# Later stores, paired weight loads, earlier heads and a sixth load buffer in one step of a retention/HGRN2 decoder layer

## The chip, the cores and the metric

The kernel runs on one core of one Trainium2 chip. The metric is the device time of one execution in microseconds; where several runs are given, it is their median. All of the time is in one launch.

## The reference, cut to what matters

The reference computes one inference step of one hybrid decoder layer (model width 1024), for one prompt of 2048 tokens with zero state and for 8 sample sequences of 8 tokens that bring a state each. Both share the weights:

```
proj = rmsnorm(x) @ w_in                      # 1024 x 4096
rq, rk, rv, rg, hq, hf, hi, hg = split(proj)  # 8 parts of 512 columns, 4 heads of 128 each
o_r = retention(rotary(rq), rotary(rk), rv)   # S = gamma_h * S + k v^T   , o = q S
o_h = hgrn2(silu(hq), 1 - f, hi, log f)       # S = diag(f) * S + (1-f) i^T, o = q S
o   = [head_rmsnorm(o_r) * silu(rg), head_rmsnorm(o_h) * silu(hg)]
x   = x + o @ w_out                           # 1024 x 1024
x   = x + square(relu(rmsnorm(x) @ w_up)) @ w_down     # 1024 x 4096, 4096 x 1024
y   = rmsnorm(x)
```

The outputs are y for prompt and samples and the final states of the 8 heads, for the prompt and for each sample sequence. Everything is in float32. The recurrences are computed in chunks: inside a chunk by products of queries and keys with a decay between them, across chunks by the state.

## The kernel before, in words

**Groups and layout.** The 2112 tokens are cut into three groups of 640 (prompt), 768 (prompt) and 704 (64 sample tokens and 640 of the prompt), worked through one after the other. Activations lie with features on the 128 partitions and tokens along the free axis, in "slabs" of 128 x 768. The mixing of all three groups (input projection, heads, output projection) comes before the three feed-forward passes, which begin at about 1170 us and multiply block matrices with fewer products by way of sums of weights (`plan_sums`, L1272) that are made beforehand, during the mixing.

**Weights in two parts.** Each 128 x 1024 weight tile is loaded into one of four `raw` buffers on SyncE's queue (L233), cast by ScalarE into a high part `hi` (L268) and subtracted by VectorE into a low part `lo` (L282, in `second_part`, four ticks after the cast). Activations have two parts as well, and each product is three matmuls: high by high, high by low, low by high. `weight(i)` makes sure that weight i is there, and brings up as many more as `self.ahead` says; `hi` and `lo` have five buffers each (`NPART`). `next_weight` hands out the next weight of the stream. For weights 4 to 35 of the first group it also stores both parts to DRAM at once (L315-316, on SyncE's queue, so the queue waits there until the low part is made); groups two and three load these parts back (L253) and do not split them again.

**Order of the work.** `mix(g)` runs over four pairs of heads, one retention head and one HGRN2 head each. For a pair, `project` makes queries, keys and forget gates (four blocks, rotary tables applied at L705-L706), `mixer` writes the side work of the pair on an agenda, and `values` (L739-L745) multiplies the tokens by the pair's four value weights (`N_VAL`). `proj` calls `tick()` after each pair of matmuls of a block's two halves, `values` after two of each three of its matmuls; `at(t, ...)` and `later(t, ...)` place a piece of side work t ticks ahead, so it is issued between the matmuls of that moment. Three 512-column matmuls of `values` are two ticks, 16 ticks a chunk of 128 tokens. Each engine then works its instructions in the order in which the program issued them (a scheduler may move them within that). The agenda of a pair holds the corner products of the HGRN2 decay levels (L983, copied out by ScalarE at L986, their exponents made on GpSimd at L901 and ScalarE at L905), the sums for the next token (their operand made at L504, the products' result taken over at L970), the retention scores (L1040, taken over by VectorE at L1041), turned keys, outputs and states.

**Heads.** When a pair's outputs exist, `cut_heads` (L1215-L1232) turns them to feature layout for the output projection: for each of its two heads and two or three chunk trios a transpose on TensorE (L1229) into a PSUM tile of the pool `mm`, which has four, then the high part on ScalarE (L1230) and the low part on VectorE (L1231). Heads of pairs 0, 1 and 2 are turned during the last pair, at ticks 50, 65 and 80; those of the last pair at its end.

**Sample states.** In the third group, `sample_states` (L775) loads each head's eight states in two halves into buffers of the pool `ld`, which has five (`NLD`), is shared with the rotary tables and the operands of the weight sums, and also holds the new states until they are stored (L849).

**The first weights.** The whole start of the kernel runs on little data: the normalising factor of the first group (`rsqrt`, L355-L356, on ScalarE), the rotary tables multiplied by it (L592, GpSimd), the first projections multiplied by it (L643, VectorE) or by the tables (L705, VectorE, which reads the PSUM tile, and L706, GpSimd), and the first blocks of weights, all within some 41 us.

Of the kernel before, what the change touches and what calls it, by code (L numbers as in the profile page):

```python
# [9 lines left out]
F32 = mybir.dt.float32  # L10
# [5 lines left out]
P = 128  # L16
# [4 lines left out]
SLEN = 8  # L21
NS = NSEQ * SLEN
# [5 lines left out]
C = 128  # L28
SLAB = 768
NSLAB = 43  # L30
NLD = 5
NRAW = 4
NPART = 5
LEVELS = (64, 32, 16, 8, 4, 2)

MASKS = (16, 8, 4, 2, "odd", 1, 0)
SMASKS = (4, 2, "odd", 1, 0)
NMSK = len(MASKS) * P + len(SMASKS) * NS
GAM = [1.0 - 2.0 ** (-5.0 - h) for h in range(H)]


# [12 lines left out]
N_VAL = 4  # L54
# [60 lines left out]
def constants():  # L115
    c = np.zeros((P, NCONST), np.float64)
    c[:, C_ID:C_ID + P] = np.eye(P)
    s = np.arange(P)[:, None]
    t = np.arange(P)[None, :]
    sc = DK ** -0.5  # L120
    same = (s // SLEN == t // SLEN) & (s < NS) & (t < NS)
    for h, g in enumerate(GAM):
        dec = np.where(s <= t, g ** np.maximum(t - s, 0), 0.0) * sc
        c[:, C_RM + h * P:C_RM + (h + 1) * P] = dec
        c[:, C_RS + h * NS:C_RS + (h + 1) * NS] = np.where(same, dec, 0.0)[:, :NS]
        c[:, C_GQ + h * P:C_GQ + (h + 1) * P] = g ** (t + 1.0)
        c[:, C_GS + h * NS:C_GS + (h + 1) * NS] = g ** (np.arange(NS) % SLEN + 1.0)
        c[:, C_KS + h] = sc * g ** (P - 1.0 - s[:, 0])
        c[:, C_KSS + h] = sc * g ** (SLEN - 1.0 - s[:, 0] % SLEN)
    c[:, C_SM:C_SM + 4] = (s % 32 // SLEN == np.arange(4)[None, :])  # L130
    def mask(w):
        if w == "odd":
            return mask(2) * (s % 2)
        return s == t if not w else (s // (2 * w) == t // (2 * w)) & (s % (2 * w) < w) & (t % (2 * w) >= w)

    m = np.concatenate([mask(w) for w in MASKS] + [(mask(w) * (s < NS))[:, :NS] for w in SMASKS], 1)
    half = DK // 2
    inv = np.power(10000.0, (-np.arange(half, dtype=np.float32) / np.float32(half)).astype(np.float64)).astype(np.float32)
    pos = in_groups(np.tile(PAST + np.arange(SLEN), NSEQ), np.arange(SEQ)).astype(np.float32)
    ang = (inv[:, None] * pos[None, :]).astype(np.float64)  # L140
    cs = np.zeros((P, 2, NT), np.float32)
    cs[:half, 0] = cs[half:, 0] = np.cos(ang)
    cs[:half, 1] = -np.sin(ang)
    cs[half:, 1] = np.sin(ang)
    return c.astype(np.float32), m.astype(np.uint8), cs.reshape(P, -1)
# [54 lines left out]
class Kernel:  # L200
# [108 lines left out]
    def next_weight(self):  # L309
        i = self.w_use  # L310
        self.w_use += 1
        r = self.weight(i)
        if N_MADE <= i < N_KEPT:
            self.kept[i] = [self.dp.tile([P, WT], F32, name=f"w{i}{part}") for part in ("hi", "lo")]
            for part, kept in zip(r, self.kept[i]):  # L315
                self.nc.sync.dma_start(kept, part.bitcast(F32))
        self.wts.pop(i - 4, None)
        return r

    def take(self, n):  # L320

# [53 lines left out]
    def build(self):  # L375
        nc, tc, I = self.nc, self.tc, self.I
        with ExitStack() as ctx:
# [33 lines left out]
            self.eps, self.eps_h = eps[:, 0:1], eps[:, 1:2]  # L411
            self.con, self.vec, self.msk = con, vec, msk
            self.mask = {w: msk[:, i * P:(i + 1) * P] for i, w in enumerate(MASKS)}
            self.smask = {w: msk[:, len(MASKS) * P + i * NS:len(MASKS) * P + (i + 1) * NS] for i, w in enumerate(SMASKS)}
            self.ident = con[:, C_ID:C_ID + P]

            gs = []
# [13 lines left out]
            self.ahead = 2  # L431
            self.weight(0)

            self.reset = cp.tile([P, P + NS], F32, name="reset")
            nc.gpsimd.memset(self.reset, 1.0)
            nc.gpsimd.memset(self.reset[:, P:].rearrange("p (c t) -> p c t", t=SLEN)[:, :, 0:1], 0.0)
            self.S = cp.tile([P, 2 * H, P], F32, name="S")
            self.AT = [cp.tile([P, 3, P], F32, name=f"AT{i}") for i in range(2)]
            for a in self.AT:
# [181 lines left out]
    def mix(self, g):  # L621
        nc = self.nc
        if g.ns:
            g.qm = [self.get(), self.get()]
            for q in g.qm:
                nc.gpsimd.memset(q, 0.0)
        g.o, g.oc = {}, {}
        end = 0
        for p in range(H):
            b = {}  # L630
            self.project(g, p, b)
            end = self.mixer(g, p, b, max(self.now, end))
            if p == H - 1:
                for q in range(H - 1):
                    self.later(50 + 15 * q, self.cut_heads, g, q)
            self.values(g, p, b)

    def block(self, g):
# [71 lines left out]
    def values(self, g, p, b):  # L710


        nc, n = self.nc, len(g.starts)
        ahead, self.ahead = self.ahead, NPART - N_VAL
        w = [self.next_weight() for _ in range(N_VAL)]
        self.ahead = ahead
        b["vs"], b["vc"], b["gate"] = None, [], []
        trios, left, i1 = [], -(-n // 3), 0
        while left:
            i0, i1 = i1, i1 - (i1 - n) // left  # L720
            left -= 1
            trios.append((i0, i1))
        g.trios = trios
        slabs = {}
        for j0 in range(0, n, 2):
            pj = self.pj.tile([P, 2, 512], F32, tag="pj", name="pjv")
            part = g.starts[j0:j0 + 2]
            for i, s in enumerate(part):
                dst = pj[:, i]
                for kb in range(KB):  # L730
                    hh, hl = g.h[kb]
                    cols = slice((kb % 2) * 512, (kb % 2 + 1) * 512)
                    wh, wl = (a[:, cols] for a in w[kb // 2])
                    if g.ns and s == 0:

                        last = kb == KB - 1
                        for q in (1, 0) if last else (0, 1):
                            if q:
                                nc.tensor.matmul(dst[:NS], hh[:, :NS], wl, start=False, stop=False, skip_group_check=True)  # L739
                            else:  # L740
                                nc.tensor.matmul(dst, self.hs[:, kb * P:(kb + 1) * P], wh, start=kb == 0, stop=last)
                        self.tick()
                        continue
                    for q, (a, ww) in enumerate(((hh, wh), (hh, wl), (hl, wh))):
                        nc.tensor.matmul(dst, a[:, s:s + C], ww, start=kb == 0 and q == 0, stop=kb == KB - 1 and q == 2)  # L745
                        if q != 1:
                            self.tick()
            for i, s in enumerate(part):
                j = j0 + i
                k = next(k for k, (a, e) in enumerate(trios) if a <= j < e)  # L750
                if k not in slabs:
                    slabs[k] = self.get(), self.get()
                c0 = (j - trios[k][0]) * 256
                for t, c in ((slabs[k][0], 0), (slabs[k][1], 256)):
                    nc.scalar.activation(t[:, c0:c0 + 256], pj[:, i, c:c + 256], AF.Copy, scale=g.rt[:, j:j + 1])
                v, z = (t[:, c0:c0 + 256] for t in slabs[k])
                b["gate"].append(z)
                if g.ns and s == 0:
                    b["vs"], b["vrows"] = (v[:, :P], v[:, P:]), v[:NS]
                    low = self.load()[:NS, :512]  # L760
                    for h, t in enumerate((v, z)):
                        nc.sync.dma_start(low[:, h * 256:(h + 1) * 256], t[NS:])
                        self.later(16 + h, lambda t=t, r=low[:, h * 256:(h + 1) * 256]: nc.vector.tensor_tensor(
                            out=t[:NS], in0=t[:NS], in1=r, op=ALU.add))
                else:
                    b["vc"].append((v[:, :P], v[:, P:]))
                if j == trios[k][1] - 1:
                    self.gates(slabs[k][1], c0 + 256, 22 if g.ns and trios[k][0] == 0 else 4)
# [97 lines left out]
    def mixer(self, g, p, b, t0):  # L866
# [15 lines left out]
        def scans():  # L882
            lf, bb = x["lf"], x["bb"]
            for c in cols:
                nc.vector.tensor_tensor_scan(out=bb[:, c], data0=self.reset[:, :C], data1=lf[:, c], initial=0.0,
                                             op0=ALU.mult, op1=ALU.add)
            if n0:
                nc.vector.tensor_tensor_scan(out=bb[:, :NS], data0=self.reset[:, P:], data1=lf[:, :NS], initial=0.0,
                                             op0=ALU.mult, op1=ALU.add)


# [269 lines left out]
        at(14, next_products)  # L1161
        at(22, next_keys)
        at(25, next_parts)
        at(50, next_to)
        for i, w in enumerate(LEVELS):
            t = 6 + step * i
            at(t, exponents, w)
# [5 lines left out]
            for sg in (parts if 2 < w < SLEN else range(2)):  # L1173
                at(t + late + 3 * sg + (wait if w == 2 else 9 if w >= 32 else 4), level, i, sg)
        for sg in parts:
            at(46 + 4 * sg, ret_scores, sg)
            at(60 + 4 * sg, turn, "ktr", rk, sg, C_KS)
        at(60, ret_queries)
        t = 6 + step * len(LEVELS)
# [677 lines left out]
```

## Time and profile before

| | |
|---|---|
| median of 3 runs | 2503.9 us (2501.46 to 2505.31) |
| the profiled execution's own time | 2503.73 us |
| its span in the profile | 2501.9 us |
| granted TensorE clock, mean | 0.997 |
| instructions | 39554 |
| TensorE busy | 99% of the span |
| VectorE, ScalarE, GpSimd busy | 73%, 49%, 15% |
| moved by DMA | 525.6 MB, 210 GB/s |

The profile is of one execution. Lines such as "PE pjv L745 <- DVE slab L705: 3.4, 1, 3.4" say that TensorE's matmuls of line 745, into the tile pjv, were idle before their start for 3.4 us in all, once, and that what ended the idle time was VectorE's instruction of line 705. In lists of single instructions the columns are start, duration, engine, line, operation, result and operands, the number of instructions in the row, and in brackets the idle time ahead of it with its releaser. "SPq" is SyncE's queue, which issues transfers. In tables by stretch, "PEclk" is the clock that TensorE was granted, as a share of full speed.

### The profile page before, as it was taken

The numbers are of one execution on the slowest core, as the hardware profiler recorded it, in microseconds if no ns is written. First come the engines' busy times: TensorE is split into PE (matmuls) and PEld (weight loads), VectorE is DVE, ScalarE is ACT, GpSimd is POOL, SyncE is SP. The second block draws the span as 40 slices with busy tenths as digits, with TensorE's granted clock in tenths as the row PEclk, the third lists the DMA queues.
The fourth block names the chain that finished last, engine by engine and source line by source line (L and its number), as shares of the span: only waits on it lengthen the run. The fifth ranks groups of instructions, "written<-read, shape, count | busy, mean of one in ns | idle before, by whom it ended". The sixth has DMA issues, their size and how long they took to land.

```text
span 2501.9 us, 39554 instructions
## 1 busy us (share of the span) xinstructions
PE 2481.5 (99%) x15408; PEld 2379.1 (95%) x15408; DVE 1814.2 (73%) x2449; ACT 1221.5 (49%) x1966; POOL 380.1 (15%) x320
## 2 busy tenths in 40 slices
PE   9999999999999999999999999999999999999998
PEld 8999898998899889989999999999999999999998
DVE  7666766557583656666775899786688878778997
ACT  6565653444463444443644555544454436445443
POOL 4223304324321443340000000000000000000000
PEclk9999999999999999999999999999999999999999
DMA  7544464645465566747866856566675555867652
GB/s 279 203 180 174 165 240 152 250 177 196 178 229 228 191 207 228 249 179 250 292 225 211 283 199 211 187 231 227 202 252 181 181 163 181 292 198 244 205 184 97
DMA packets 191968, 525.57 MB, mean 210 GB/s; under 512 B 21027, under 2 KB 62883, under 8 KB 191782
## 3 DMA queue, kind: packets, MB, share of 16 engines
q1 hardware_dynamic: 191638, 523.03, 60.8%
q8 instruction: 121, 1.98, 0.3%
q14 instruction: 65, 0.53, 0.1%
q10 hardware_dynamic: 144, 0.02, 0.0%
HBM read 389.28 MB, written 132.39 MB: 209 GB/s over the span
## 4 chain that ended last, share of the span: by engine, by line
PE 92%; DVE 2%; POOL 2%; DMA 1%; ACT 1%; issue 1%; SPq 0%; DVEq 0%; POOLq 0%; ACTq 0%
PE pf L1240 26%; PE pj L1240 25%; PE pj L339 20%; PE pjv L745 12%; PE mm L926 2%; PE mm L1108 1%; PE mm L1110 1%; PE mm L1116 1%; DMA raw<-w 1%; PE mm L983 1%; PE mm L1229 1%; PE mm L856 1%; PE mm L790 1%; PE mm L1040 1%; POOL slab L901 0%
## 5 line engine op out<-in xcount | busy, mean ns | idle before, releaser
L268 ACT CAST hi<-raw 128x1024 fp32r<-128x1024 f32 x392 | 411.8, 1051 | 608.3 <-PE pf L1240 242.1
L1240 PE MATMUL pf<-slab,hi 128*128 128x320 f32 (+2 forms) x2768 | 657.8, 321 | 0.0
L1240 PE MATMUL pj<-slab,hi 128*128 128x352 f32 (+2 forms) x2608 | 620.7, 322 | 0.0
L282 DVE TENSOR_TENSOR lo<-raw,hi 128x1024 fp32r<-128x1024 f32 x392 | 482.9, 1233 | 120.8 <-ACT hi L268 116.0
L339 PE MATMUL pj<-slab,hi 128*128 128x320 f32 (+2 forms) x2304 | 486.6, 327 | 0.8 <-DVE slab L1300 0.8
L1240 PEld LDWEIGHTS pf<-slab,hi 128*128 128x128 f32 x2768 | 480.1, 188 | 0.0
L1240 PEld LDWEIGHTS pj<-slab,hi 128*128 128x128 f32 x2608 | 452.9, 188 | 0.1
L1240 PE MATMUL pf<-slab,lo 128*128 128x320 f32 (+2 forms) x1384 | 444.2, 321 | 0.0
L1240 PE MATMUL pj<-slab,lo 128*128 128x352 f32 (+2 forms) x1304 | 419.2, 321 | 0.0
L339 PEld LDWEIGHTS pj<-slab,hi 128*128 128x128 f32 x2304 | 382.0, 188 | 5.0 <-issue 1.9
L745 PE MATMUL pjv<-hi,slab 128*128 128x512 f32 x1024 | 349.1, 403 | 3.4 <-DVE slab L705 3.4
L339 PE MATMUL pj<-slab,lo 128*128 128x320 f32 (+2 forms) x1152 | 282.3, 326 | 0.1
L1240 PEld LDWEIGHTS pf<-slab,lo 128*128 128x128 f32 x1384 | 259.7, 188 | 0.0
L1240 PEld LDWEIGHTS pj<-slab,lo 128*128 128x128 f32 x1304 | 244.7, 188 | 0.0
L745 PEld LDWEIGHTS pjv<-hi,slab 128*128 128x128 f32 x1024 | 194.1, 190 | 40.3 <-DVE slab L705 3.6
L745 PE MATMUL pjv<-lo,slab 128*128 128x512 f32 x512 | 206.7, 404 | 0.0
L339 PEld LDWEIGHTS pj<-slab,lo 128*128 128x128 f32 x1152 | 198.3, 188 | 0.5 <-DVE lo L282 0.4
L1331 ACT CAST slab<-slab 128x640 fp32r<-128x640 f32 (+2 forms) x192 | 145.2, 778 | 69.5 <-DVE slab L1342 50.4
L1335 DVE TENSOR_TENSOR slab<-slab 128x640 fp32r<-128x640 f32 (+2 forms) x192 | 166.8, 887 | 13.4 <-PE pf L1240 6.6
L905 ACT ACTIVATE slab<-slab 128x640 f32<-128x640 f32 (+2 forms) x72 | 56.3, 782 | 125.0 <-POOL slab L901 124.1
L745 PEld LDWEIGHTS pjv<-lo,slab 128*128 128x128 f32 x512 | 97.1, 190 | 15.3 <-DVE lo L282 0.3
L1585 DVE TENSOR_TENSOR slab<-pf,slab 128x640 f32<-128x640 f32 (+2 forms) x88 | 77.7, 888 | 22.0 <-PE pf L1240 21.5
(231 smaller groups left out, 2959.5 us busy)
## 6 DMA issues: line engine op xcount, KB each, us to landing
raw<-w SPq DMA_DIRECT2D x264, 512.0 KB, 4.6
slab<-u SPq DMA_DIRECT2D x32, 384.0 KB, 5.0
u<-ld SPq DMA_DIRECT2D x30, 384.0 KB, 4.3
slab<-u SPq DMA_DIRECT2D x32, 352.0 KB, 5.1
u<-ld SPq DMA_DIRECT2D x30, 352.0 KB, 4.4
slab<-u SPq DMA_DIRECT2D x32, 320.0 KB, 4.5
u<-ld SPq DMA_DIRECT2D x30, 320.0 KB, 4.0
ld<-x SPq DMA_DIRECT2D x16, 384.0 KB, 4.0
```

What stands on the lines that cost most here:

```text
L268: self.nc.scalar.copy(hi, raw)
L282: self.nc.vector.tensor_tensor(out=lo, in0=self.second.pop(j), in1=hi.bitcast(F32), op=ALU.subtract)
L339: self.nc.tensor.matmul(pj[:, i, :T2], w, a[:, c0:c1], start=j == 0 and q == 0, stop=j == n - 1 and q == 2)
L745: nc.tensor.matmul(dst, a[:, s:s + C], ww, start=kb == 0 and q == 0, stop=kb == KB - 1 and q == 2)
L790: nc.tensor.matmul(po, g.qm[i][:, s * NS:(s + 1) * NS], s0[i][:, s * P:(s + 1) * P], start=False, stop=i == 1 and s == 3)
L856: nc.tensor.transpose(ps[:, j * P:(j + 1) * P], src[:, c], self.ident)
L905: nc.scalar.activation(x["dd", w][:, a:T], x["dd", w][:, a:T], AF.Exp)
L926: nc.tensor.matmul(ps[:, j], qk[:, cols[c]], second(qk[:, cols[c]]), start=True, stop=True)
L1240: self.nc.tensor.matmul(*a, **k)
L1331: self.nc.scalar.copy(hi[:, :g.T], B[name][:, :g.T])
L1335: self.nc.vector.tensor_tensor(out=lo[:, :g.T], in0=B[name][:, :g.T], in1=hi.bitcast(F32)[:, :g.T], op=ALU.subtract)
L1585: nc.vector.tensor_tensor(out=r, in0=ps, in1=r, op=ALU.add)
```

## The change

Six edits, all in the order and the buffers of the work; no product and no arithmetic is added or left out.

1. The stores of the weights kept for the later groups go on the agenda ten ticks ahead (`keep`), and are no longer issued at the moment when a weight is handed out.
2. `values` asks for the pair's last but one value weight, with those that `self.ahead` adds, in one call before it takes the four.
3. Heads of pairs 0, 1 and 2 are turned at ticks 4, 16 and 28 of the last pair, not 50, 65 and 80.
4. The pool `ld` has six buffers instead of five.
5. Inside the pair's agenda the next-token sums go to tick 45 (from 50) and the retention scores to 48 + 4 sg (from 46 + 4 sg).
6. The masks of the sample tokens are cut from those of the prompt, so the mask table that is loaded has 896 columns instead of 1216; the scans read an existing tile of ones, and the tile of ones and zeros for the samples' scans loses its 128 columns of ones.

```diff
-NLD = 5
+NLD = 6
...
-NMSK = len(MASKS) * P + len(SMASKS) * NS
+NMSK = len(MASKS) * P
...
         if N_MADE <= i < N_KEPT:
             self.kept[i] = [self.dp.tile([P, WT], F32, name=f"w{i}{part}") for part in ("hi", "lo")]
-            for part, kept in zip(r, self.kept[i]):
-                self.nc.sync.dma_start(kept, part.bitcast(F32))
+            self.later(10, self.keep, r, self.kept[i])
         self.wts.pop(i - 4, None)
         return r
+
+    def keep(self, parts, kept):
+        for part, k in zip(parts, kept):
+            self.nc.sync.dma_start(k, part.bitcast(F32))
...
-            self.reset = cp.tile([P, P + NS], F32, name="reset")
+            self.reset = cp.tile([P, NS], F32, name="reset")
...
             if p == H - 1:
                 for q in range(H - 1):
-                    self.later(50 + 15 * q, self.cut_heads, g, q)
+                    self.later((4, 16, 28)[q], self.cut_heads, g, q)
             self.values(g, p, b)
...
         ahead, self.ahead = self.ahead, NPART - N_VAL
+        self.weight(self.w_use + N_VAL - 2)
         w = [self.next_weight() for _ in range(N_VAL)]
...
-                nc.vector.tensor_tensor_scan(out=bb[:, c], data0=self.reset[:, :C], data1=lf[:, c], initial=0.0,
+                nc.vector.tensor_tensor_scan(out=bb[:, c], data0=self.ones, data1=lf[:, c], initial=0.0,
...
-        at(50, next_to)
+        at(45, next_to)
...
-            at(46 + 4 * sg, ret_scores, sg)
+            at(48 + 4 * sg, ret_scores, sg)
```

More of the change, by code (lines that the diff above doesn't have):

```diff
@@ L36 @@
 MASKS = (16, 8, 4, 2, "odd", 1, 0)
-SMASKS = (4, 2, "odd", 1, 0)
-NMSK = len(MASKS) * P + len(SMASKS) * NS
+NMSK = len(MASKS) * P
 GAM = [1.0 - 2.0 ** (-5.0 - h) for h in range(H)]
@@ L134, in mask @@
         return s == t if not w else (s // (2 * w) == t // (2 * w)) & (s % (2 * w) < w) & (t % (2 * w) >= w)
-    m = np.concatenate([mask(w) for w in MASKS] + [(mask(w) * (s < NS))[:, :NS] for w in SMASKS], 1)
+    m = np.concatenate([mask(w) for w in MASKS], 1)
     half = DK // 2
@@ L413, in build @@
             self.mask = {w: msk[:, i * P:(i + 1) * P] for i, w in enumerate(MASKS)}
-            self.smask = {w: msk[:, len(MASKS) * P + i * NS:len(MASKS) * P + (i + 1) * NS] for i, w in enumerate(SMASKS)}
+            self.smask = {w: m[:, :NS] for w, m in self.mask.items() if w != "odd" and w <= SLEN // 2 or w == "odd"}
             self.ident = con[:, C_ID:C_ID + P]
@@ L432, in build @@
             self.weight(0)
-            self.reset = cp.tile([P, P + NS], F32, name="reset")
+            self.reset = cp.tile([P, NS], F32, name="reset")
             nc.gpsimd.memset(self.reset, 1.0)
-            nc.gpsimd.memset(self.reset[:, P:].rearrange("p (c t) -> p c t", t=SLEN)[:, :, 0:1], 0.0)
+            nc.gpsimd.memset(self.reset.rearrange("p (c t) -> p c t", t=SLEN)[:, :, 0:1], 0.0)
             self.S = cp.tile([P, 2 * H, P], F32, name="S")
@@ L884, in scans @@
             for c in cols:
-                nc.vector.tensor_tensor_scan(out=bb[:, c], data0=self.reset[:, :C], data1=lf[:, c], initial=0.0,
+                nc.vector.tensor_tensor_scan(out=bb[:, c], data0=self.ones, data1=lf[:, c], initial=0.0,
                                              op0=ALU.mult, op1=ALU.add)
             if n0:
-                nc.vector.tensor_tensor_scan(out=bb[:, :NS], data0=self.reset[:, P:], data1=lf[:, :NS], initial=0.0,
+                nc.vector.tensor_tensor_scan(out=bb[:, :NS], data0=self.reset, data1=lf[:, :NS], initial=0.0,
                                              op0=ALU.mult, op1=ALU.add)
```

## The prediction

> **What bounds the kernel now.** I read the page first, then who TensorE waited for, then the granted clock in narrow stretches around the longest waits, then each engine's instructions in order of time at those places.
>
> ```profile
> PE 2481.5 (99%) x15408; PEld 2379.1 (95%) x15408; DVE 1814.2 (73%) x2449; ACT 1221.5 (49%) x1966; POOL 380.1 (15%) x320
> ...
> L1240 PE MATMUL pf<-slab,hi 128*128 128x320 f32 (+2 forms) x2768 | 657.8, 321 | 0.0
> ```
>
> TensorE is busy for 2481.5 of 2501.9 us, and the feed-forward products (L1240), which fill the span from about 1170 us on, wait for nothing. The change removes no matmul. So all it can win is idle time of TensorE in the first half, and what hangs on it.
>
> ```profile
> engine line waited for: us in total, times, longest us
> PE pjv L745 <- DVE slab L705: 3.4, 1, 3.4
> PE mm L1229 <- DVE slab L1041: 1.8, 1, 1.8
> PE mm L790 <- DMA ld<-hg_s: 1.6, 2, 1.4
> PE mm L1040 <- ACT AT L986: 1.3, 3, 0.6
> ...
> PE mm L1229 <- DVE AT L970: 0.4, 1, 0.4
> PE mm L983 <- DVE slab L912: 0.3, 1, 0.3
> ```
>
> These waits lie before 1200 us. Five places, 8.8 us in all, are ones that the edits touch: the first value product (3.4), the early heads of the last group's last pair (1.8 and 0.4), the states of the sample sequences (1.6), retention scores in the second group (1.3), one corner product (0.3). Two of them cost more than their idle time:
>
> ```profile
> core 0: us, PE busy (x), PEclk, DMA share, GB/s
> 36.50:41.30 4.80, 1.45 (x8) 1.00 1.03 327
> 41.30:44.80 3.50, 3.50 (x10) 0.51 0.72 286
> ...
> 1092.70:1096.00 3.30, 1.08 (x7) 1.00 1.03 322
> 1096.00:1099.50 3.50, 3.50 (x18) 0.51 0.99 365
> ```
>
> Behind both stalls the granted clock is 0.51 for 3.5 us, so half of that, about 1.7 us, is lost again each time. The ceiling is 8.8 + 3.4 = 12.2 us.
>
> **The change part by part.** Stores ten ticks later, and a pair's value weights asked for together: this is the first stall.
>
> ```profile
> 27.87 0.33 SPq L316 DMA_DIRECT2D w4lo<-lo  x1
> 28.24 0.43 SPq L233 DMA_DIRECT2D raw<-w  x1
> ```
>
> ```profile
> 28.67 0.51 ACT L355 ACTIVATE slab<-mm,eps 128x320 f32<-128x320 f32 x1
> 33.08 1.05 ACT L268 CAST hi<-raw 128x1024 fp32r<-128x1024 f32 x1 [3.91 <-DMA raw<-w]
> 34.03 0.47 ACT L356 ACTIVATE slab<-slab 128x320 f32<-128x320 f32 x1
> ```
>
> ```profile
> 17.06 1.23 DVE L282 TENSOR_TENSOR lo<-raw,hi 128x1024 fp32r<-128x1024 f32 x1 [1.96 <-ACT hi L268]
> ...
> 26.62 2.36 DVE L282 TENSOR_TENSOR lo<-raw,hi 128x1024 fp32r<-128x1024 f32 x2
> ...
> 35.30 4.28 DVE L643 TENSOR_TENSOR slab<-slab 128x640 f32<-128x640 f32 x2
> 39.51 0.81 DVE L705 TENSOR_TENSOR slab<-pj,ld 128x640 f32<-128x640 f32 x1
> ```
>
> ```profile
> 36.57 0.46 PE L339 MATMUL pj<-slab,lo 128*128 128x320 f32 x2
> 40.37 0.50 PE L745 MATMUL pjv<-hi,slab 128*128 128x512 f32 x1 [3.35 <-DVE slab L705]
> ```
>
> Read backwards: TensorE waits for a PSUM buffer that L705 frees at 40.32. L705 needs the rotary table, which needs the whole normalising factor. Its second half (L356) stands on ScalarE behind a weight cast (L268) that waits 3.91 us for a load. SyncE could issue that load (third value weight) only at 28.24, since the store of w4's low part, ahead of it on its queue, waited for w4's subtraction, the first of the two in the row at 26.62, and so went at 27.87. In the new order three loads precede the stores. The load then goes when its buffer is free, with the subtraction that ends at 17.06 + 1.23 = 18.3, and lands 33.08 - 28.24 = 4.8 us later, at 23.1. Its cast (1.05) now stands ahead of L355 and is done by about 25.3; L356 follows at 28.67 + 0.51 and ends at 29.7, not 34.5. The cast of the fourth value weight comes behind it, so nothing is late there.
>
> From 34.50 to 40.32 the rest of the chain took 5.8 us: it would end at 35.5. But the order puts the low part of the fourth value weight ahead of L705. That adds 1.2 us (17.06), or about twice as much if GpSimd slows it as it slowed the L643 pair: 36.7 to 38.1. TensorE is through its block at 36.9. A stall of 0 to 1.2 us is left; I take 0.7, near the middle, since GpSimd's table work runs at that time. With no 3 us gap I expect no slow stretch. The gain is 3.4 - 0.7 + 1.7 = 4.4 us, between 3.9 and 5.1. The corner product's 0.3 goes too: its chain starts some 5 us earlier, TensorE 4.4. The delayed stores keep their buffers 10 ticks (about 3.4 us) longer, and SyncE's queue then holds them behind three loads; the next user of such a buffer comes five weights later, so the wait lies beside matmuls (if that cover went, a cast would be late by 3.4 us).
>
> ```profile
> 34.58 4.32 POOL L592 TENSOR_TENSOR ld<-ld,slab 128x640 f32<-128x640 f32 x2 [10.62 <-ACT slab L356]
> 38.98 2.00 POOL L706 TENSOR_TENSOR slab<-slab,ld 128x640 f32<-128x640 f32 x1
> ```
>
> Two L643 took 4.28 us while GpSimd ran L592. The Trainium skill, "SBUF — State Buffer", section "SBUF: two separate sides", says that a VectorE instruction with two SBUF inputs and a GpSimd instruction share a port pair that one of them holds for its whole instruction. By that rule the fourth low part stands behind L706 (2.00) whenever GpSimd starts first, and the stall left is 1.2 us and the sum 0.5 us smaller; if VectorE starts first it is 0. The trace agrees as far as the doubled L643 shows.
>
> Six load buffers: the states.
>
> ```profile
> 872.93 0.42 SPq L849 DMA_DIRECT2D hg_so<-ld  x1
> ...
> 874.54 0.39 SPq L775 DMA_DIRECT2D ld<-hg_s  x1
> ```
>
> The second hg_s load of a pair waited for a buffer and went out behind the state stores; TensorE needed it at once. In the new order both hg_s loads of a pair stand ahead of all four state stores, over 10 us earlier. I count the whole 1.6 us. Beyond 1170 us the sixth buffer only moves operand loads forward, where TensorE has no wait (L1240, 0.0): nothing.
>
> Ticks 45 and 48: the retention scores.
>
> ```profile
> 501.09 0.85 ACT L905 ACTIVATE slab<-slab 128x768 f32<-128x768 f32 x1 [2.09 <-POOL slab L901]
> ```
>
> ```profile
> 502.19 0.94 PE L1040 MATMUL mm<-slab 128*128 128x128 f32 x6 [0.37 <-ACT AT L986]
> ```
>
> The second score product needs the PSUM tile that L986 frees, which stands behind a decay that waits for GpSimd. Two ticks are 0.7 us (three 512-column matmuls), more than the longest of these waits (0.6). The 1.3 us go. The next-token sums come 5 ticks, 1.7 us, earlier; their operand (L504) is done over 3 us before in such a pair, so nothing is added there.
>
> Heads at ticks 4, 16 and 28: the last pairs.
>
> ```profile
> core 0: us, PE busy (x) PEld busy (x) DVE busy (x) ACT busy (x) POOL busy (x), PEclk, DMA share, GB/s
> 655.00:672.00 17.00, 17.00 (x84) 13.66 (x83) 12.80 (x16) 6.40 (x11) 12.63 (x9) 1.00 0.86 310
> 1071.00:1089.00 18.00, 18.00 (x85) 13.95 (x84) 13.92 (x17) 6.32 (x11) 13.13 (x10) 1.00 0.36 137
> ```
>
> ```profile
> 668.84 0.56 PE L983 MATMUL mm<-slab 128*64 128x64 f32 x6
> ...
> 676.39 1.47 PE L1229 MATMUL mm<-con,slab 128*128 128x128 f32 x12
> ...
> 1085.53 0.45 PE L983 MATMUL mm<-slab 128*64 128x64 f32 x4
> ```
>
> ```profile
> 677.54 2.19 DVE L1231 SCALAR_TENSOR_TENSOR slab<-mm,vec,slab 128x384 fp32r<-128x384 f32 x4 [0.39 <-ACT slab L1230]
> ...
> 1116.45 2.07 DVE L1231 SCALAR_TENSOR_TENSOR slab<-mm,vec,slab 128x320 fp32r<-128x320 f32 x4 [0.40 <-ACT slab L1230]
> ```
>
> The work is the same; only the place moves. In the last group the old place cost 1.8 + 0.4 + 1.7 = 3.9 us. The new place puts three batches of four evacuations (2.2, 2.1 us of VectorE each, and about as much of ScalarE) into a stretch where VectorE is busy for 13 of 17 us. All four PSUM tiles go to a batch, so what follows on TensorE waits for VectorE. TensorE itself reaches the first corner product (L983) later by three batches of 1.4 us, 4.2 us. Second group: up to L504 VectorE has about 11 us of work from 657.4, with the batches 17.8, end 675.2, first tile free 1.6 earlier at 673.6; TensorE comes at 668.84 + 4.2 = 673.0, so 0.6 us is lost. Last group: the steps in the new order add to 19 us from 1073.0, first tile free at 1090.5 against 1085.53 + 4.2 = 1089.7: 0.8 us, and then about 0.9 us for the tile of the next-token sums, whose mask copies stand behind two more products of the next decay level. First group, with no weight sums on VectorE: 0. Bounds for the three together: 0 (GpSimd, freed of the overlap with weight sums, delivers its exponents earlier) and 5 us (VectorE's idle time all filled, 2 us each in two groups, 1 in the first). I take 2.3.
>
> At nothing: the smaller mask load (its first reader is 20 us behind it), scans that read the tile of ones (same instruction and size), the shorter memset before the first matmuls.
>
> **The sum**, against the profiled execution's 2503.7 us (span 2501.9; the median of the runs is 2503.9, the same): 4.4 + 0.3 + 1.6 + 1.3 + 3.9 - 2.3 = 9.2 us. Forecast 2494.5 us.
>
> **The rivals.** (1) *The first stall stays for the most part.* L705 also waits for GpSimd's tables, and doubled VectorE and GpSimd instructions could push it out by 3 us; the slow stretch comes back. Against it: that chain starts 4.8 us earlier. Then 3.4 + 1.7 of the gain go, less what the earlier loads still save (1): 2498.6. (2) *New waits in the last pairs take back what the old ones gave.* For it: 12.8 to 13.9 us of VectorE work already there. At the far end 5 us are lost, and stalls of 2.2 us within 3.4 us were enough for a slow stretch at 1096, so two such add 3.4: 12.2 - 0.7 - 8.4, 2500.6, within 0.2%. (3) *Slower:*
>
> ```profile
> 664.50 0.85 ACT L905 ACTIVATE slab<-slab 128x768 f32<-128x768 f32 x1 [6.27 <-POOL slab L901]
> ```
>
> ScalarE holds a batch's evacuation behind a decay that waits for GpSimd (here it idled 6.27 us for one). If each later batch waited for one such decay, TensorE would lose about 4 us twice in each of three pairs, with a slow stretch of 1.7 behind each pair: 3 x (8 + 1.7) = 29, less 11.5 won: 2521. It decides from about 4 us per pair and batch; the order has the decay ahead of the second batch, but TensorE reaches the third batch some 5 us later, which covers it. (4) *Better:* no new wait and no stall left at the start, 12.2: 2491.5, and with smaller waits of the same stretch gone (0.8 at 351, 0.6 at 1158) 2490. That the edits don't act is excluded by the instruction order, which shows the loads and the heads moved.
>
> The Trainium skill, "TensorE: Matmul & The Clock Gate", section "Part 1: The HAM clock gate (the "warmup" mystery)", lets the clock fall only after an idle window of about 3.4 us. The row 1092.70:1096.00 speaks otherwise: TensorE was busy for 1.08 of 3.30 us and the clock fell. By the page rival 2 would cost 3.4 us less, 2497.2.
>
> **How the numbers follow.** Forecast, 2491.8 to 2498: 0.66. Rival 1: 0.10. Rival 2: 0.12. Rival 3: 0.03. Rival 4: 0.09. 0.2% (5 us) is about what a measurement of this kernel can tell from no change. Faster by over 0.2% means under 2498.7: the forecast, rival 4, half of rival 1 and a fifth of rival 2 give 0.82. Slower: rival 3 and a little for the unforeseen, 0.04. Within: 0.14. The range takes in rival 4, the forecast, rival 1 and most of rival 2: 2489.5 to 2500.5.
>
> **What would show it.** After: no wait of the first value product over 1.3 us and a clock of 1.00 at 41 us; the third value load issued near 18 us and L356 done near 30; no wait for hg_s; no slow stretch near 1096, and the waits at L983 or L1229 of the last pairs under 1 us each. A new wait of TensorE for L1231's tiles of over 2 us in a pair, or a clock of 0.5 in a last pair, would make it wrong; so would a first stall that only moved to another releaser.

## The result and the profile after

The changed kernel takes 2490.97 us (median of 4 runs, 2490.0 to 2491.32) against 2503.13 us before (4 runs, 2501.46 to 2505.31): ratio 0.995, 95% interval 0.9933 to 0.9968. That is 12.2 us where 9.2 were forecast; it lies inside the range, below the forecast's own range (2491.8 to 2498), at the number of rival 4 (2491.5). The interval is a gain of 8 to 17 us, so the times alone do not tell 9.2 from 12.2; the terms have to be checked in the traces. The profiled span went from 2501.9 to 2489.4 us, by 12.5.

Busy times of the changed kernel, part 1 of its page, and then whom TensorE waited for:

```profile
PE 2475.5 (99%) x15408; PEld 2376.1 (95%) x15408; DVE 1807.9 (73%) x2449; ACT 1223.6 (49%) x1966; POOL 372.6 (15%) x320
```

```profile
engine line waited for: us in total, times, longest us
PE mm L408 <- DVE eps L412: 1.1, 1, 1.1
PE pj L341 <- DVE slab L1303: 0.8, 1, 0.8
PE mm L1113 <- DVE S L1126: 0.7, 1, 0.7
PE mm L512 <- DVE slab L506: 0.6, 1, 0.6
PE pjv L748 <- DVE slab L707: 0.5, 1, 0.5
PE pj L341 <- DVE lo L281: 0.4, 1, 0.4
PE pf L1787 <- ACT slab L1778: 0.4, 1, 0.4
PE mm L816 <- ACT slab L813: 0.4, 1, 0.4
PE pj L341 <- ACT hi L267: 0.2, 1, 0.2
```

Lines are those of the changed kernel, two or three above the old ones. The list adds up to 5.1 us, before to 11.9. The first value product (L748, before L745) waits 0.5 and not 3.4 us; the waits for sample states, for the PSUM tiles of turned heads and for the scores are not in the list at all. Four short waits, 1.6 us together, are new in the list: L512 (0.6), L816 (0.4) and two of L341 for the parts of a weight (0.4 and 0.2). TensorE has the same 15408 matmuls and 6.0 us less busy time; about 3.4 us of that is the half clock, since no stretch runs at it any more (stretches of the changed kernel, columns as before):

```profile
core 0: us, PE busy (x) PEld busy (x) DVE busy (x) ACT busy (x) POOL busy (x), PEclk, DMA share, GB/s
37.00:41.00 4.00, 3.48 (x17) 2.73 (x16) 3.72 (x5) 3.92 (x6) 2.74 (x3) 1.00 1.03 402
41.00:45.00 4.00, 4.00 (x20) 3.30 (x19) 3.17 (x8) 1.47 (x2) 1.46 (x2) 1.00 0.98 345
...
1090.00:1096.00 6.00, 6.00 (x44) 4.95 (x43) 2.96 (x7) 1.72 (x5) 2.46 (x4) 1.00 0.60 189
1096.00:1100.00 4.00, 4.00 (x22) 3.40 (x21) 0.59 (x3) 0.14 (x2) 0.00 (x0) 1.00 0.00 0
```

So 6.8 us of listed waits and about 3.4 us of half clock make 10.2 of the 12.5 us. The other 2.3 are not gaps: TensorE's idle time fell by only 6.5 us (20.4 to 13.9), no more than the listed waits. They are matmuls that last less at a clock of 1.00 in both kernels (6.0 - 3.4 = 2.6 us of busy time); why is not taken apart.

The first stall went as the prediction had it. SyncE's queue, then VectorE, in the changed kernel:

```profile
15.60 12.84 SPq L232 DMA_DIRECT2D raw<-w  x4
28.50 0.42 SPq L320 DMA_DIRECT2D w4hi<-hi  x1
```

```profile
30.28 4.34 DVE L645 TENSOR_TENSOR slab<-slab 128x640 f32<-128x640 f32 x2
34.53 2.60 DVE L281 TENSOR_TENSOR lo<-raw,hi 128x1024 fp32r<-128x1024 f32 x1
37.06 0.81 DVE L707 TENSOR_TENSOR slab<-pj,ld 128x640 f32<-128x640 f32 x1
```

Four loads pass before the first store. The fourth low part still stands ahead of L707 and takes 2.60 us; L707 ends at 37.87, inside the forecast's 36.7 to 38.1, and 0.5 us of wait is left where 0.7 were taken. ScalarE was done with L358 (L356 before) at 30.15, near the 29.7 of the forecast.

### The profile page after: what moved, and what is told of

It reads as the page before. It is cut to its first block, busy times and chain, and to the rows that moved or that the text cites. A ratio compares the mean times of both kernels' runs of the same rounds, so it can differ in the third digit from the quotient of the medians.

```text
span 2489.4 us, 39552 instructions
## 1 busy us (share of the span) xinstructions
PE 2475.5 (99%) x15408; PEld 2376.1 (95%) x15408; DVE 1807.9 (73%) x2449; ACT 1223.6 (49%) x1966; POOL 372.6 (15%) x320
## 4 chain that ended last, share of the span: by engine, by line
PE 96%; DVE 1%; ACT 1%; DMA 1%; issue 0%; POOL 0%; SPq 0%; DVEq 0%; POOLq 0%
PE pf L1243 26%; PE pj L1243 25%; PE pj L341 21%; PE pjv L748 14%; PE mm L929 2%; PE mm L1111 1%; PE mm L1113 1%; PE mm L1119 1%; PE mm L986 1%; PE mm L1232 1%; PE mm L1043 1%; PE mm L793 1%; PE mm L859 1%; PE mm L512 0%; PE mm L511 0%; DVE lo L281 0%
## 5 line engine op out<-in xcount | busy, mean ns | idle before, releaser
L341 PE MATMUL pj<-slab,hi 128*128 128x320 f32 (+2 forms) x2304 | 484.7, 327 | 1.0 <-DVE slab L1303 0.8
L341 PEld LDWEIGHTS pj<-slab,hi 128*128 128x128 f32 x2304 | 381.7, 188 | 4.8 <-issue 1.4
L748 PE MATMUL pjv<-hi,slab 128*128 128x512 f32 x1024 | 345.4, 400 | 0.5 <-DVE slab L707 0.5
L341 PE MATMUL pj<-slab,lo 128*128 128x320 f32 (+2 forms) x1152 | 282.3, 326 | 0.5 <-DVE lo L281 0.4
L748 PEld LDWEIGHTS pjv<-hi,slab 128*128 128x128 f32 x1024 | 192.5, 188 | 36.1 <-PE pj L341 0.8
L748 PE MATMUL pjv<-lo,slab 128*128 128x512 f32 x512 | 205.0, 400 | 0.0
L341 PEld LDWEIGHTS pj<-slab,lo 128*128 128x128 f32 x1152 | 198.3, 188 | 1.0 <-DVE lo L281 1.0
L1338 DVE TENSOR_TENSOR slab<-slab 128x640 fp32r<-128x640 f32 (+2 forms) x192 | 166.8, 886 | 14.8 <-PE pf L1243 6.9
L748 PEld LDWEIGHTS pjv<-lo,slab 128*128 128x128 f32 x512 | 96.6, 189 | 14.7
L1275 DVE TENSOR_TENSOR raw<-raw 128x1024 f32<-128x1024 f32 x64 | 93.6, 1462 | 0.3
```

Source lines behind the costliest of these rows:

```text
L341: self.nc.tensor.matmul(pj[:, i, :T2], w, a[:, c0:c1], start=j == 0 and q == 0, stop=j == n - 1 and q == 2)
L1275: self.tc.keep_in_program_order(nc.vector.tensor_tensor(out=x[into], in0=x[a], in1=x[b], op=op))
L1338: self.nc.vector.tensor_tensor(out=lo[:, :g.T], in0=B[name][:, :g.T], in1=hi.bitcast(F32)[:, :g.T], op=ALU.subtract)
```

## The experiments

The kernel before was run beside each set: 2503.26, 2502.48 and 2501.95 us (medians of 15, 14 and 21 runs, all between 2499.4 and 2506.9). The changed kernel's four runs lie within 1.3 us. The before-medians differ by as much from set to set, so differences of about 1 us between sets are not told from nothing by the times. Edit 6, the smaller tables, was not run alone. Names that begin with u or s are the changed kernel with something undone, b the kernel before with something added.

| run | what | us | against |
|---|---|---|---|
| u_heads | heads back at 50, 65, 80 | 2492.69 | +1.7 to changed |
| u_start | both edits of the first loads undone | 2495.74 | +4.8 |
| u_ld5 | five load buffers | 2495.84 | +4.9 |
| u_ticks | next-token sums 50, scores 46 | 2491.28 | +0.3 |
| u_both | u_heads and u_ticks together | 2496.41 | +5.4 |
| s_stores | stores at once, joint request kept | 2490.27 | -0.7 |
| s_joint | stores later, no joint request | 2490.48 | -0.5 |
| p_sbuf | low parts of heads from an SBUF copy | 2491.97 | +1.0 |
| b_heads | early heads alone | 2499.17 | -2.8 to before |
| b_ld6 | sixth buffer and its smaller tables alone | 2501.78 | -0.2 |
| b_again | the kernel before, one run | 2505.53 | |
| i_ticks | s_joint, sums 47, scores 50 | 2491.06 | +0.1 to changed |

**First loads.** u_start:

```diff
-            self.later(10, self.keep, r, self.kept[i])
+            self.keep(r, self.kept[i])
...
-        self.weight(self.w_use + N_VAL - 2)
```

> The changed kernel with the stores of kept parts at once and without the joint request of the value weights. Theory A: the first value product waits 3.4 us again near 37 us and the clock falls to about 0.5 for 3.5 us behind it; 3.4 - 0.5 + 1.7 + 0.3 = 4.9 us come back, 2495.9 us. Rival B (the stall comes back but the clock does not fall, since the fall had another cause): 3.2 us, 2494.2 us.

4.8 us came back: the wait is 3.1 us and the clock falls behind it (stretches of u_start):

```profile
37.00:40.30 3.30, 0.35 (x3) 0.09 (x1) 3.30 (x4) 2.96 (x4) 3.22 (x2) 0.97 0.94 270
40.30:43.80 3.50, 3.39 (x9) 2.68 (x10) 1.81 (x3) 3.45 (x5) 3.50 (x3) 0.54 0.99 356
```

Theory A holds, rival B (no fall of the clock) does not. s_stores and s_joint each take back one of these two edits:

> The changed kernel with the stores of kept parts issued at once, the joint request of the value weights kept. Theory A (either of the two edits alone puts the three loads ahead of the first store on SyncE's queue): nothing changes, 2491.0 us, first value product waits under 1 us. Rival B (the delay is what removes the stall): the third load goes out near 28 us, the wait of 3 us and the low clock are back, 2495.7 us.

> The changed kernel without the joint request of the value weights, the stores still ten ticks later. Theory A (either edit alone is enough): 2491.0 us, first value product waits under 1 us. Rival B (the joint request is what removes the stall, since it also moves the casts and low parts ahead): 2495.7 us.

Neither made the kernel slower. SyncE's queue in s_stores, where the stores are not delayed:

```profile
15.49 10.01 SPq L232 DMA_DIRECT2D raw<-w  x3
25.59 0.38 SPq L320 DMA_DIRECT2D w4hi<-hi  x1
```

The joint request alone issues three loads before any store, the delay alone four. Each edit does the whole work; the other one adds nothing that these runs can tell.

**Heads and ticks.** u_heads and u_ticks:

```diff
-                    self.later((4, 16, 28)[q], self.cut_heads, g, q)
+                    self.later(50 + 15 * q, self.cut_heads, g, q)
```

> The changed kernel with the heads of the last pairs back at ticks 50, 65 and 80; all else as changed. Theory A (what the trace of the changed kernel suggests: the early heads cost nothing, since VectorE's low parts read PSUM and leave GpSimd's exponents alone): the whole 3.9 us of the old place comes back, 2494.9 us against 2491.0, with a wait of over 1.5 us for the tiles of the turned heads near 1085 us and a stretch of granted clock near 0.5 behind it. Theory B (the sum of the prediction: 3.9 us won, 2.3 us lost again in the other pairs): 1.6 us come back, 2492.6 us. Rival C (the 2.2 us of idle time at that place were chance of one execution): no stall, 2491.

```diff
-        at(45, next_to)
+        at(50, next_to)
...
-            at(48 + 4 * sg, ret_scores, sg)
+            at(46 + 4 * sg, ret_scores, sg)
```

> The changed kernel with the next-token sums at tick 50 and the retention scores at 46, 50, 54. Theory A: the score products wait for ScalarE's copies again, three times, 1.3 us, and the 0.6 us wait of a next-token sum near 993 us, which the changed kernel has, goes: 2491.0 + 1.3 - 0.6 = 2491.7 us. Rival B (the waits of the score products were gone anyway, since the early heads moved them): only the 0.6 us go, 2490.4 us.

u_heads came out at the number of theory B, but not for its reason. In the changed kernel TensorE waits in no last pair for the tiles of turned heads or of the corner products behind them. One other wait goes with the early heads: L816 waits 0.2 to 0.4 us for ScalarE's L813 near 1100 us in all nine profiles with early heads, and in none of the five without. So 0.4 of the 2.3 us are seen. It was the old place that cost less: in u_heads the waits for turned heads are 1.3 us in all, the longest 0.6, and the clock stays at 1.00. u_ticks came out 0.4 us under theory A, and its 0.3 us over the changed kernel are not told from nothing. In its profile, taken of the longest of its five executions (2492.79), two waits of score products are back, 1.1 us together, and the next-token wait is gone. So both edits were undone:

> The changed kernel with both the heads (50, 65, 80) and the ticks of the pair's agenda (next-token sums 50, scores 46 + 4 sg) as before. Undone singly they cost 1.7 and 0.3 us (2492.69 and 2491.28 against 2490.97). Theory A (each edit alone takes the collision away, in which turned heads, scores and next-token sums want the four PSUM tiles at the same ticks, so neither undoing alone shows its price): both together cost 3.9 for the heads' place and 1.3 for the scores, near 2496 us, and the stretch of low clock near 1090 us is back. Rival B (the two add): 1.7 + 0.3, 2493.0 us, no low clock.

5.4 us, where the single undoings add to 2.0. The size is that of theory A, the place is not. Waits of u_both, two of its rows, then its stretches near the end of the last pair:

```profile
PE mm L1113 <- DVE S L1126: 2.3, 1, 2.3
PE mm L1043 <- ACT AT L989: 1.2, 3, 0.4
...
PE mm L1232 <- DVE AT L973: 0.4, 1, 0.4
```

```profile
1146.00:1149.00 3.00, 0.76 (x6) 0.57 (x4) 3.00 (x5) 0.29 (x2) 0.00 (x0) 1.00 0.69 209
1149.00:1153.00 4.00, 3.92 (x17) 3.92 (x18) 3.04 (x10) 3.41 (x9) 0.00 (x0) 0.57 0.95 351
```

The scores wait three times again. Turned heads near 1085 us wait 0.3 and 0.4 us only. The large stall and the half clock sit 60 us later, at the last state update, which VectorE reaches late:

```profile
1144.59 1.22 DVE L281 TENSOR_TENSOR lo<-raw,hi 128x1024 fp32r<-128x1024 f32 x1 [2.98 <-ACT hi L267]
1145.74 1.22 DVE L1275 TENSOR_TENSOR raw<-raw 128x1024 f32<-128x1024 f32 x1
1146.87 0.82 DVE L1338 TENSOR_TENSOR slab<-ld,slab 128x640 fp32r<-128x640 f32 x1
1147.61 1.22 DVE L1275 TENSOR_TENSOR raw<-raw 128x1024 f32<-128x1024 f32 x1
1148.74 0.28 DVE L1126 SCALAR_TENSOR_TENSOR S<-S,mm 128x128 f32<-128x128 f32 x1
```

L1126 (0.28 us) stands behind a weight's low part and three pieces of work for the coming feed-forward pass, two weight sums and L1338. VectorE idled 2.98 us just before, for a weight's high part. In the changed kernel the same spot costs 0.7 us: there L1338 ran at 1140.06, ahead of that idle time, and the L1126 that TensorE needs came between the two sums.

Why was the old place cheap here and dear in the kernel before? The trace of before, VectorE and GpSimd, against u_both at the same instructions:

```profile
1092.40 1.82 DVE L912 TENSOR_TENSOR slab<-slab 128x320 f32<-128x320 f32 x1
```

```profile
1092.31 1.56 POOL L1045 TENSOR_TENSOR slab<-slab,con 128x640 f32<-128x640 f32 x1 [1.99 <-PE mm L1040]
```

```profile
1084.06 0.47 DVE L915 TENSOR_TENSOR slab<-slab 128x320 f32<-128x320 f32 x1
```

```profile
1084.14 1.79 POOL L1048 TENSOR_TENSOR slab<-slab,con 128x640 f32<-128x640 f32 x1 [2.16 <-PE mm L1043]
```

L915 is L912 of before. Where GpSimd started 0.09 us ahead, VectorE's product lasted 1.82 us, to 0.35 us behind GpSimd's end; where VectorE started 0.08 us ahead, it took 0.47. The score evacuation behind it releases the PSUM tile that the turned heads wait for. If the two kernels differ in nothing else there, 1.35 us of the 1.8 us stall hang on 0.1 us. To see whether it changes between executions:

> The kernel before, unchanged, for a second profile. Theory A (the 1.8 us wait and the low clock behind it near 1092 us are a matter of which of VectorE's L912 and GpSimd's L1045 starts first, since the same order of work with both early heads and ticks undone took 0.47 us for that instruction instead of 1.82): in about half of the executions L912 takes some 0.5 us, the wait is about 0.3 us and the clock stays at 1.00; the span is then near 2498.5 us, otherwise again 2502. Rival B (the stall belongs to the order of the work): 1.8 us and the low clock again, 2502.

It did not: L912 took 1.82 us again, with the same 1.8 us wait and the low clock; b_ld6, with the sixth buffer, shows the same. Three profiles with the old start agree, so the sixth buffer alone does not move it; that the edits of the start do, alone or with it, is open. u_heads does not bear on it: its later scores put L1048 at 1088.36, well behind L915 (1083.92, 0.47 us).

At another place the records show both outcomes. The changed kernel and u_ticks have the same instructions in the same order on VectorE, ScalarE and GpSimd up to 36 us. GpSimd in the changed kernel, then VectorE and GpSimd in u_ticks:

```profile
30.23 3.70 POOL L594 TENSOR_TENSOR ld<-ld,slab 128x640 f32<-128x640 f32 x2 [6.02 <-ACT slab L358]
```

```profile
30.20 2.94 DVE L645 TENSOR_TENSOR slab<-slab 128x640 f32<-128x640 f32 x2
```

```profile
30.25 4.33 POOL L594 TENSOR_TENSOR ld<-ld,slab 128x640 f32<-128x640 f32 x2 [6.13 <-ACT slab L358]
```

Where GpSimd started 0.05 us ahead, VectorE's two L645 took 4.34 us (their row stands with the first stall above); where VectorE started 0.05 us ahead, 2.94. The first value product then waits 0.5 us in the one and not at all in the other. u_heads and u_both go with u_ticks. s_joint and i_ticks, again with equal instructions up to 36 us, differ in the same way: VectorE 0.05 us ahead, 2.94 us and no wait; GpSimd 0.39 us ahead, 4.32 us and 0.9 us of wait. (In s_stores the starts lie 0.01 us apart, and the pair took 2.93.) With one profile of each kernel it is not shown whether two executions of one kernel can differ in this.

b_heads is the kernel before with the heads moved alone:

> The kernel before with only the heads at ticks 4, 16 and 28. Theory A (edits of heads and ticks cover each other; with the old ticks the heads' place is worth 2496.4 - 2491.3 = 5.1 us, and the early batches cost nothing): about 2502.5 - 5.1 = 2497.4 us, no wait above 0.5 us for turned heads, low clock only near 41 us. Theory B (the prediction's net for the heads): 1.6 us won, 2501 us, with new waits of 0.8 us and 0.9 us in the last group's last pair.

2.8 us were won (ratio 0.9991, interval 0.9982 to 1.0, so 0 to 4.5 us), between the two theories: the interval holds theory B's 1.6 and ends short of theory A's 5.1. In the profile the span fell by 4.1 us (2497.8): the stall and the half clock near 1092 us are gone, and the new waits that theory B expected are not there. Two small waits go against theory A: 0.7 us at the end of the last pair for the last outputs (L1149), 0.2 before, and 0.4 us at L813, which is L816 of the changed kernel. The rest of what is missing is not found.

**Why the early heads cost next to nothing.** VectorE and GpSimd in the second group's last pair, changed kernel:

```profile
654.89 2.16 DVE L1234 SCALAR_TENSOR_TENSOR slab<-mm,vec,slab 128x384 fp32r<-128x384 f32 x4
...
664.80 0.56 DVE L506 TENSOR_TENSOR slab<-slab 128x384 fp32r<-128x384 f32 x1 [0.63 <-ACT slab L505]
```

```profile
655.11 0.83 POOL L903 TENSOR_TENSOR slab<-slab 128x384 f32<-128x384 f32 x1 [2.01 <-DVE slab L888]
655.90 0.84 POOL L904 TENSOR_TENSOR slab<-slab 128x384 f32<-128x384 f32 x1
```

and GpSimd at this place before:

```profile
661.22 1.72 POOL L900 TENSOR_TENSOR slab<-slab 128x384 f32<-128x384 f32 x1 [1.94 <-DVE slab L885]
662.91 1.56 POOL L901 TENSOR_TENSOR slab<-slab 128x384 f32<-128x384 f32 x1
```

Beside the evacuations, whose one operand is in PSUM, GpSimd's products take 0.83 us; before, they took 1.72 beside a weight sum (L1272) and 1.56 beside the rotary product L707, which both read two slabs of SBUF. From the start of L707 at 651.22 to the end of L506 passed 14.1 us with two batches in it, before 13.1 us with none. p_sbuf gives VectorE two SBUF operands:

```diff
+                f = self.get()
+                self.tc.keep_in_program_order(nc.scalar.copy(f[:, :e - a], ps))
-                nc.vector.scalar_tensor_tensor(out=lo[:, a:e], in0=ps, scalar=w, in1=hi.bitcast(F32)[:, a:e],
+                nc.vector.scalar_tensor_tensor(out=lo[:, a:e], in0=f[:, :e - a], scalar=w, in1=hi.bitcast(F32)[:, a:e],
```

> The changed kernel with one ScalarE copy more for each turned head's part: the PSUM tile is copied to SBUF, and VectorE makes the low part from the copy, so that it reads two operands of SBUF; the result is the same. It adds four ScalarE copies of some 0.5 us to each batch, and frees PSUM tiles sooner or as soon. Theory A (the early heads cost nothing because VectorE's low parts read PSUM and leave GpSimd its full pace): GpSimd's products of 384 columns (L903, L904) beside the batches take 1.1 us or more, no longer 0.83, the operand of the next-token sums comes over 1 us later, and TensorE waits for it, 0.5 to 2 us in each of the last pairs of groups two and three: 2492 to 2495 us. Rival B (GpSimd's pace has nothing to do with where VectorE reads; it was fast since a weight sum had been moved away): the durations stay at 0.83 and the time at 2491 us, within what the copies on ScalarE cost.

```profile
654.99 1.89 POOL L903 TENSOR_TENSOR slab<-slab 128x384 f32<-128x384 f32 x1 [2.03 <-DVE slab L888]
656.85 1.15 POOL L904 TENSOR_TENSOR slab<-slab 128x384 f32<-128x384 f32 x1
```

```profile
656.12 3.77 DVE L1236 SCALAR_TENSOR_TENSOR slab<-slab,vec 128x384 fp32r<-128x384 f32 x3
...
667.03 0.55 DVE L506 TENSOR_TENSOR slab<-slab 128x384 fp32r<-128x384 f32 x1
```

GpSimd's products go to 1.89 and 1.15 us, three low parts take 3.77 us (four took 2.16), and L506 ends 16.5 us after L707 began (651.06 here), 2.4 later. L903's 1.89 us are in part beside L709 (655.25 to 656.20), a product of two slabs that the order moved up here; L904's 1.15 stand beside the low parts alone, while ScalarE idled (655.30 to 658.03). So GpSimd's slower pace is not the doing of ScalarE's copies, and rival B is out. TensorE then waits 0.6 us for L915 and 0.4 for L989 in this group, not for the next-token operand that theory A named, and the third group shows no new wait. The kernel is 1.0 us slower, or 1.5 to 1.7 against s_joint and s_stores of the same set, the edge of what theory A expected; ScalarE's copies are part of this price.

**The sixth buffer.** u_ld5 (`NLD = 5`):

> The changed kernel with five load buffers. Theory A: the states of the sample sequences are late again, 1.6 us of waits for hg_s, 2492.6 us. Rival B (the other edits moved the loads or the products so that five do as well): no wait for hg_s, 2491.0 us. Rival C (the buffer is also short where sums of weights are made): over 2493.

The waits for states are back, and larger than before:

```profile
PE mm L793 <- DMA ld<-hg_s: 2.9, 2, 2.7
```

The late load landed 6.2 us after its issue, in the kernel before 5.1. The profiles of u_ld5 and the changed kernel differ by 4.3 us: TensorE idles 2.9 us more (16.8 against 13.9), and its matmuls are busy 1.4 us longer at a clock of 1.00, which is not taken apart. Alone on the kernel before the same edit won nothing:

> The kernel before with only the sixth load buffer, and the smaller tables that make room for it. Theory A (what five buffers cost depends on how long the late load of a sample state takes to land, 1.4 us of wait in one execution and 2.7 in another, plus about 1 us of smaller gaps where products of states stand between those of the projection): 3 to 5 us won, 2498.5 us, no wait for hg_s. Theory B (the prediction): 1.6 us won, 2501 us.

```profile
PE mm L1109 <- DVE S L1122: 2.1, 1, 2.1
```

The ratio is 1.0006 (0.9997 to 1.0014); both theories miss. No wait for hg_s is left, but the last state update (L1109, L1110 in the kernel before, where it waited 0.6 us) now waits 2.1 us, as in u_both. In this profile, which is 2.0 us longer than the median of its runs, what is won at 878 us is given back at 1156 us. With six buffers and the heads in the old place that wait is 2.1, 2.3 (u_both) and 1.2 us (u_heads); with five buffers it is 0.6 and 0.4 (before, b_again), and with early heads at most 0.7 at a time, with five buffers or six.

**A further step.** i_ticks is s_joint with

```diff
-        at(45, next_to)
+        at(47, next_to)
...
-            at(48 + 4 * sg, ret_scores, sg)
+            at(50 + 4 * sg, ret_scores, sg)
```

> The changed kernel without the joint request, with the next-token sums at tick 47 (not 45) and the retention scores at 50 + 4 sg (not 48). Theory A: the 0.6 us wait for the operand of the next-token sums near 993 us goes, and no wait of the score products comes back: 0.6 us under the kernel without the joint request (2490.5), so 2489.9 us, inside what a measurement can tell; the trace decides. Rival B: the wait only moves to the scores or to the turned keys behind them, 2490.5 us or above.

2491.06 us. The next-token wait is gone from the trace, and the scores do not wait, but the first value product waits 0.9 us (the two L645 took 4.32 us here) and the last state update 0.7. Rival B, by another path; nothing beats the changed kernel by more than a measurement can tell.

## Why the prediction was right, and where it was not

- *First stall, 4.4 + 0.3.* Right, with its mechanism: undone together 4.8 us come back. That two edits were needed was not claimed, and is not so. The 0.7 us left of the stall were a middle value: the profiles with this start show 0 to 0.9, by which of VectorE and GpSimd starts first at 30 us.
- *Half clock behind two stalls, 1.7 each.* Right at the first place (u_start). The second is bound to the stall at 1092 us and went with it; u_both shows the same behind another stall.
- *Early heads: 3.9 won, 2.3 lost.* The step that failed is the one where the batches' VectorE time was added to the 11 us of work up to L504, to end at 17.8. That adds 6.8 us, about three batches. Only two, 4.3 us, stand ahead of L506, the third follows at 665.28, and the stretch grew by 1.0 us. The two filled idle time of VectorE (1.62 and 0.49 us before L911, 0.63 before L506 after), and the SBUF products behind them ran in 0.55 us where they had taken 1.2, since GpSimd's share was done beside the batches and GpSimd then idled (662.81 to 665.44). The lower bound of 0 named this reason; the middle value was the wrong pick. The traces show 0.4 us of the 2.3, at L816, which the prediction did not name.
- *Ticks, 1.3, and states, 1.6.* The waits were there and went. What they are worth alone is another matter: undone, the ticks cost 0.3 us, not told from nothing, and the buffer 4.9; added alone, the buffer won nothing that can be measured. The terms do not add: heads and ticks cost 5.4 us together, 1.7 and 0.3 singly; and the start, the heads with the ticks, and the buffer, undone in turn, cost 15.1 us, more than the 12.2 won.
- *New waits.* The sentence that the next-token operand was done over 3 us before was wrong for the third pair of the last group: 0.6 us of wait (L512 <- L506).
- *The total.* In the profiles the terms came to 4.6 for the start (forecast 4.4), 0.3, 1.6, 1.3 and 3.9, less 0.4 at L816 and 1.1 for waits that the sum did not have (L512, L341, L1113, less 0.2 that went at L1229): 10.2. The other 2.3 us are the shorter matmuls, which no term named. So 1.9 us of the difference is the mis-sized term; that the total lies so near rival 4's 12.2 is partly luck.
- *Rivals.* The time is that of rival 4, but not its conditions: 0.5 us of the first stall is left, and new waits came. Rival 1 did not come, nor did rival 3: TensorE waited for no evacuation of turned heads. Rival 2's new waits did not show; its half clock, and the stalls of 2 us that bring it, exist in the kernels with the heads in the old place.

## What to carry to other kernels

Price a piece of moved work by the operands it reads and not by its duration alone: here an evacuation from PSUM left GpSimd's product at 0.83 us, and work of VectorE on two SBUF tiles took it to 1.15 and more. Where several edits clear the same collision, undo them singly and together. A wait that goes may come back at the next place where the same engine is late. If two edits have one mechanism, test whether one is enough.

## What the runs showed of the hardware

- VectorE and GpSimd on SBUF: with about 0.1 us of difference in which of the two started first, one VectorE product of 320 columns took 0.47 or 1.82 us, and a pair of 640 columns 2.94 or 4.34. The Trainium skill, "SBUF — State Buffer", section "SBUF: two separate sides", has one of the two hold the shared port for a whole instruction; by that rule the product waits for GpSimd's end, and the trace agrees (the product ends at 1094.22, GpSimd at 1093.87).
- The granted clock fell to 0.57 behind 3.0 us in which TensorE was busy for 0.76 (u_both), and did not fall behind 3.0 us with 0.37 (u_ld5). The longest single idle time was 2.3 us in the first and 2.7 in the second. The stretches of u_ld5:

```profile
871.00:874.00 3.00, 0.37 (x4) 0.18 (x2) 0.00 (x0) 0.00 (x0) 0.00 (x0) 1.00 1.01 388
874.00:876.00 2.00, 1.91 (x13) 1.76 (x14) 0.00 (x0) 0.81 (x6) 0.76 (x1) 1.00 0.14 57
```

How long TensorE idles does not decide it alone; what else does is open.
